# Reordering the first half's triangular substitution in the recurrent block of a two-layer decoder trunk on one core

## The chip, the cores and the metric

The kernel runs on one core of one Trainium2 chip. The metric is the device time of one execution in microseconds (us). Before the change the median of three runs is 2140.88 us (2133.08 to 2142.15).

## What is computed

The program is a trunk of two layers over 512 tokens of width 1024. Each layer is a half SwiGLU block, a mixer and another half SwiGLU block. Layer 0 mixes by attention, layer 1 by RWKV-7. Only the RWKV-7 mixer is touched:

```
xx = shift(h) - h;   xr, xw, xk, xv, xa, xg = [h + xx * mix[i] for i in range(6)]
r, k, v = xr @ w_r, xk @ w_k, xv @ w_v
decay = exp(-exp(-softplus(-(w0 + tanh(xw @ w1) @ w2)) - 0.5));  a = sigmoid(a0 + (xa @ a1) @ a2)
S_t = S_{t-1} (diag(decay_t) - kk_t^T (kk_t * a_t)) + v_t k_t^T;   y_t = S_t r_t      (16 heads of 64)
```

The kernel doesn't step through the tokens. It works in chunks of 64 tokens and, in each chunk and head, needs the inverse of a unit triangular 64 x 64 matrix of "ties" between the chunk's tokens.

## The kernel before

The heads are worked in two halves of eight (`sg` 0 and 1, four head pairs `j` each). Ahead of the recurrence stand three projections, each as two halves of 512 output columns: K, V, R. `project(half, ...)` runs over eight pieces k of the contraction; for k = 0 to 5 it issues 12 matmuls (4 blocks of 128 by 3 split products, L120, tile rm) and yields, then the pieces 6 and 7 block by block with two more yields. These are steps 0 to 7. `weave` resumes side generators after named steps of a projection, so side work sits between the matmuls. Matmuls keep their written order (`pinned`). On the other engines a scheduler orders the instructions by its own timeline, and `after(ins, dep)` adds a constraint of order to it.

The side generators that matter:

- `rw_own_ties` (L1542, L1552): per pair 16 small matmuls (tile rq) make the ties, VectorE masks them into `us`, and the SyncE queue (SP) stores them to DRAM as `lin` in four transfers of 32 KB: 16 for a half.
- `rw_inverse` (L1591 to L1616): SP loads `lin` back as one 512 KB tile with one 32 x 32 triangle per partition, GpSimd presets T, and VectorE substitutes in 31 steps of two operations each (L1601 product, L1607 sum). Then T and its transposed copy U go out to DRAM (ScalarE copy L1616), come back, and two rounds of 32 x 32 matmuls finish the 64 x 64 inverse.
- `rw_decay` (L1492 to L1497): per pair six matmuls into two rq banks (there are three), which ScalarE empties by two tanh (line 102, `us` and `pa`), then a VectorE scan (L1495) and two exponentials on ScalarE (line 102 again).
- `evac_v` (L1356 to L1364): V's eight blocks are copied by ScalarE, centred by GpSimd, and stored by SP as `vd` and `vcd`, 256 KB each.
- `mixed` (L1321 to L1334): makes each token-shifted input piece: ScalarE scale, VectorE add (L1323), ScalarE cast (L1332), and the low part on GpSimd or VectorE (L1334). R mixes its eight pieces anew for each half.

R and K, V weights were split earlier and lie in DRAM; SP loads them back piece by piece (L288, 512 KB each, tile parts) into a ring of four slots. SP issues all of the above in one order, so a transfer that waits holds those behind it. VectorE and ScalarE work in order too.

In the kernel before, the first half's ties come after steps 3 to 6 of V's first half, and the whole of its substitution is resumed after step 7.

Of the kernel before, what the change touches and what calls it, by code (L numbers as in the profile page):

```python
# [14 lines left out]
ALU = mybir.AluOpType  # L15
# [34 lines left out]
class Trunk:  # L50
    def __init__(self, ctx, tc, aps):
        self.tc, self.nc, self.a = tc, tc.nc, aps
        nc = self.nc
        self.cp = ctx.enter_context(tc.tile_pool(name="const", bufs=1))
        self.sb = ctx.enter_context(tc.tile_pool(name="work", bufs=1))
        self.ps = ctx.enter_context(tc.tile_pool(name="banks", bufs=1, space=PSUM))
        self.dram = ctx.enter_context(tc.tile_pool(name="dram", bufs=1, space=DRAM))

        n_x = N_CONST + NCH * S
        self.call, self.cpos = self.cp.tile([P, n_x + 4096], F32, name="const"), 0  # L60
        self.x_all, self.raw_all = self.shaped(self.call[:, N_CONST:n_x], [NCH, S]), self.call[:, n_x:]
        self.parts_all = self.cp.tile([P, 8192], F32R, name="parts")
        self.x = [self.x_all[:, c, :] for c in range(NCH)]
        self.ident = self.c("ident", [P])
        make_identity(nc, self.ident)
        self.ones = self.c("ones", [P], 1.0)

        self.blk = self.c("blk", [P], 0.0)
        for h in range(2):
            nc.gpsimd.memset(self.blk[h * 64 : (h + 1) * 64, h * 64 : (h + 1) * 64], 1.0)  # L70
        self.consts = {}
        self.wlist, self.wring, self.wblocks, self.plan_ring = [], [], [], "f"

        self.wloads, self.slot_last, self.fops, self.n_ffn = [], {}, {}, 0
        self.extra, self.extra_for = None, 0

        self.wkeep = {}

        self.parked_w, self.park_ops, self.park_turn = {}, [], 0
        self.wload = self.wconv = self.wpos = 0  # L80
        self.wcv = {}
        self.n_conv = 0

        self.fcol = self.c("fcol", [4, 4])
        self.conv_ahead, self.limit = 2, 1 << 30
        self.last_mm = self.turned = self.gate = None

        self.pinned, self.last_pe = False, None
        self.parking = False
        self.table, self.table_ins, self.preload = None, [], None  # L90
# [1207 lines left out]
    def rwkv(self, gain):  # L1298
        nc, mm = self.nc, self.nc.tensor.matmul
# [46 lines left out]
        vd = self.dram.tile([4, P, D], F32, name="vd")  # L1346
        vcd = self.dram.tile([4, P, D], F32, name="vcd")

        def evac_v(half, ps):


            e = lambda z: z.rearrange("p (h d) -> p h d", d=C)
            for b in range(4):
                t, tc = self.row("v", 4), self.row("vc", 2)
                mean = self.vmean[:, half, b, :]
                nc.scalar.copy(t, ps[b])  # L1356
                nc.vector.tensor_reduce(out=mean, in_=e(t), axis=AX.X, op=ALU.add)
                nc.scalar.mul(mean, mean, 1.0 / C)
                nc.gpsimd.tensor_tensor(
                    out=e(tc), in0=e(t), in1=mean[:, :, None].to_broadcast([P, 8, C]), op=ALU.subtract  # L1360
                )
                cs = slice(half * S, (half + 1) * S)
                nc.sync.dma_start(vd[b][:, cs], t)
                nc.sync.dma_start(vcd[b][:, cs], tc)  # L1364

        def project(half, xm, evac, natural, i_mix=None):

# [50 lines left out]
        weave(project(0, xm, evac_k, False, 2), ((6, 7), decay))  # L1418
        weave(project(1, xm, evac_k, False), ((0, 1), decay), ((0, 1, 2), norm), ((6, 7), keys))
        xm = {}  # L1420
        ties, norm, inverse = self.rw_own_ties(0), self.rw_norm(1), self.rw_inverse(0, None)
        weave(project(0, xm, evac_v, True, 3), ((0, 1), keys), ((0, 1, 2), norm), ((3, 4, 5, 6), ties), ((7,), inverse))
        weave(project(1, xm, evac_v, True))
        decay, keys, ties = self.rw_decay(1), self.rw_keys(1), self.rw_own_ties(1)
        bonus = []
        evac_r = lambda half, ps: bonus.append(self.rw_prep2(half, ps))

        weave(project(0, None, evac_r, False, 0), ((2, 3, 4, 5), decay), ((6, 7), keys))
        weave(
            project(1, None, evac_r, False, 0),  # L1430
            ((0, 1), keys), ((2, 3, 4, 5), inverse), ((4, 5, 6, 7), ties), ((6, 7), bonus[0]),
        )
        recur = self.rw_recur(0)
        next(recur)
        inverse = self.rw_inverse(1, None)
        weave(recur, ((6, 7), bonus[1]), ((2, 5, 8, 11, 14, 20, 21, 22, 23), inverse))
        self.limit = len(self.wlist)
        self.rw["g2"] = self.next_w()
# [33 lines left out]
    def rw_decay(self, sg):  # L1472
# [5 lines left out]
        for j in range(4):  # L1478
# [13 lines left out]
            nc.scalar.activation(pi, pi, AF.Identity, bias=self.const(1.0))  # L1492
            self.act(self.rw_rate(j), ps[1], AF.Tanh, scale=0.5, bias=col("a0"))
            runs = self.runs.rearrange("p c t -> p (c t)")
            nc.vector.tensor_tensor_scan(out=cum, data0=runs, data1=pi, initial=0.0, op0=ALU.mult, op1=ALU.add)  # L1495
            self.act(pr, cum, AF.Exp, scale=-0.5 * E_HALF)
            self.act(pi, cum, AF.Exp, scale=0.5 * E_HALF)  # L1497
            yield
# [81 lines left out]

    halves = [(slice(h * 64, h * 64 + 64), slice(64 - h * 64, 128 - h * 64)) for h in range(2)]

    def rw_inverse(self, sg, dep):

        nc, mm = self.nc, self.mm
        rw = self.rw
# [2 lines left out]
        inv = self.x_all[:, :4].rearrange("p (n i) s -> p n (i s)", n=2) if sg else self.shaped(self.raw_all[:, :2048], [2, 1024])  # L1589
        L, T, pt = inv[:, 0, :], inv[:, 1, :], self.rows[:, 2:].rearrange("p i s -> p (i s)")  # L1590
        load = nc.sync.dma_start(L, rw["lin", sg])  # L1591
        U, t0, L = L, pt, big(L)
        self.after(nc.gpsimd.memset(T, 0.0), load)
        nc.gpsimd.memset(T[:, 0::33], 1.0)
# [2 lines left out]
        for i in range(31):  # L1597
# [5 lines left out]
                in1=T[:, i : i + 1, :j].to_broadcast([P, n, j]), op=ALU.mult,  # L1603
            )
            if done == 0:
                self.after(ins, self.newed if sg else dep)
            nc.vector.tensor_tensor(out=T[:, j:, :j], in0=T[:, j:, :j], in1=pv, op=ALU.add)  # L1607

            done += 2 * n * j + 250
            if sg and done > 3740:  # L1610
                done = 0
                yield
        dt = self.dram.tile([P, 1024], F32, name=f"tout{sg}")
        du = self.dram.tile([P, 1024], F32, name=f"uout{sg}")
        nc.sync.dma_start(dt.rearrange("p (i t) -> p i t", i=32), T)
# [312 lines left out]
```

## Time and profile before

| | |
|---|---|
| three runs, median (range) | 2140.88 us (2133.08 to 2142.15) |
| profiled execution, its own time | 2135.13 us |
| its span, mean granted TensorE clock | 2133.2 us, 0.987 |
| TensorE busy | 2048.1 us (96%) |
| VectorE busy | 1585.9 us (74%) |
| ScalarE, GpSimd busy | 954.4 us (45%), 123.4 us (6%) |

The profiled execution lies inside the range of the runs, 5.75 us under their median. Times inside it are counted from the span's start. V's projection runs from about 1447 to 1506, R's from about 1504 to 1583; the recurrence follows.

### The profile page before, as it was taken

Reading aid. Unit: us, or ns where it says so; the run is one execution under the profiler, and the core shown is the slowest. Engines: PE = TensorE matmul, PEld = TensorE weight load, DVE = VectorE, ACT = ScalarE, POOL = GpSimd, SP = SyncE. Lnnn points to the kernel's source line nnn. Section 1 sums busy time; section 2 is a strip of 40 time slices with the busy share of each in tenths; the row PEclk is TensorE's granted clock in tenths of the full one; section 3 lists DMA queues with packets and bytes.
Section 4 is the critical chain, followed back from the end, with each engine's and each line's share of the span. In section 5 each row is a group of like instructions: output and inputs, shape, how many; then the busy total and the mean of one; then the engine's idle time right before and its main releaser. Section 6 shows DMA issues by size and latency. Waiting matters only on the chain.

```text
span 2133.2 us, 29169 instructions
## 1 busy us (share of the span) xinstructions
PE 2048.1 (96%) x11527; PEld 1639.8 (77%) x11527; DVE 1585.9 (74%) x1981; ACT 954.4 (45%) x1381; POOL 123.4 (6%) x165
## 2 busy tenths in 40 slices
PE   8999999999989999999999999999898999999998
PEld 6788888776877788877878888777566668888887
DVE  6778786467777888887798888556966557887784
ACT  5433443354335554444544444373634425433342
POOL 0000000211000000000000000112322100000000
PEclk9999999999989999999999999999989999999999
DMA  5333332421113468763255674536654332333321
GB/s 169 89 115 103 99 99 72 125 79 51 52 47 100 147 221 275 237 207 128 62 196 197 211 235 158 207 112 191 213 135 104 91 120 83 109 99 119 109 89 40
DMA packets 219296, 282.41 MB, mean 132 GB/s; under 512 B 45395, under 2 KB 135659, under 8 KB 219160
## 3 DMA queue, kind: packets, MB, share of 16 engines
q1 hardware_dynamic: 216520, 278.20, 41.4%
q10 hardware_dynamic: 2640, 2.36, 0.3%
q8 instruction: 91, 1.49, 0.3%
q14 instruction: 45, 0.37, 0.1%
HBM read 227.76 MB, written 54.59 MB: 132 GB/s over the span
## 4 chain that ended last, share of the span: by engine, by line
PE 77%; DVE 11%; DMA 5%; ACT 3%; issue 2%; SPq 1%; POOL 0%; DVEq 0%; ACTq 0%
PE fp L120 36%; PE fd L120 18%; PE am L120 7%; PE rm L120 4%; PE rq L120 2%; DVE parts L297 2%; PE wo L120 2%; DMA const<-in_ffn_w_up_dram 1%; PE rl L120 1%; PE rr L120 1%; DVE const L1601 1%; DVE wx L293 1%; DVE const L1607 1%; ACT parts L296 1%; PE fd L691 1%
## 5 line engine op out<-in xcount | busy, mean ns | idle before, releaser
L120 PE MATMUL fp<-parts,xs 128*128 128x512 f32 x2016 | 493.1, 393 | 13.2 <-DVE parts L297 9.0
L120 PEld LDWEIGHTS fp<-parts,xs 128*128 128x128 f32 x2016 | 377.6, 189 | 96.6 <-DVE parts L297 12.0
L120 PE MATMUL fd<-act,parts 128*128 128x512 f32 x1728 | 409.4, 390 | 2.5 <-DVE acts L332 1.6
L296 ACT CAST parts<-wx 128x1024 fp32r<-128x1024 f32 x224 | 233.6, 1051 | 349.9 <-PE fp L120 174.6
L120 PEld LDWEIGHTS fd<-act,parts 128*128 128x128 f32 x1728 | 323.7, 188 | 72.6 <-DVE acts L332 3.4
L297 DVE TENSOR_TENSOR parts<-wx,parts 128x1024 fp32r<-128x1024 f32 x224 | 271.8, 1220 | 73.2 <-ACT parts L296 73.1
L296 ACT CAST parts<-const 128x1024 fp32r<-128x1024 f32 (+1 forms) x192 | 198.2, 1033 | 262.0 <-PE fp L120 134.0
L120 PE MATMUL fp<-parts,xb 128*128 128x512 f32 x1152 | 291.3, 400 | 9.6 <-ACT wx L668 6.8
L297 DVE TENSOR_TENSOR parts<-const,parts 128x1024 fp32r<-128x1024 f32 (+1 forms) x192 | 229.5, 1197 | 59.4 <-ACT parts L296 54.3
L120 PEld LDWEIGHTS fp<-parts,xb 128*128 128x128 f32 x1152 | 216.8, 191 | 56.1 <-ACT wx L668 7.4
L654 DVE TENSOR_TENSOR wx<-fp,wx 128x1024 f32<-128x1024 f32 x140 | 168.7, 1218 | 30.0 <-PE fp L120 28.8
L712 DVE SCALAR_TENSOR_TENSOR const<-fd,const 128x512 f32<-128x512 f32 x160 | 108.4, 685 | 77.6 <-PE fd L120 77.4
L120 PE MATMUL fp<-parts,xa 128*128 128x512 f32 x576 | 145.0, 400 | 4.3 <-ACT xa L572 2.6
L120 PEld LDWEIGHTS fp<-parts,xa 128*128 128x128 f32 x576 | 110.2, 193 | 29.2 <-ACT xa L572 3.3
L120 PE MATMUL am<-xg,parts 128*128 128x512 f32 x384 | 99.4, 410 | 0.0
L416 POOL TENSOR_TENSOR ssum<-ssum,sq 128x512 f32<-128x512 f32 x14 | 23.0, 1646 | 1198.3 <-ACT sq L415 1197.9
L120 PEld LDWEIGHTS am<-xg,parts 128*128 128x128 f32 x384 | 72.0, 191 | 25.6 <-issue 9.9
L102 ACT ACTIVATE wx<-wx,const 128x512 f32<-128x512 f32 x80 | 53.5, 716 | 43.7 <-DVE wx L654 43.6
L242 ACT CAST acts<-wx 128x1024 fp32r<-128x1024 f32 (+2 forms) x37 | 37.1, 1004 | 68.4 <-DMA wx<-in_rw_wk_dram 18.3
L243 DVE TENSOR_TENSOR acts<-wx,acts 128x1024 fp32r<-128x1024 f32 (+2 forms) x37 | 42.9, 1162 | 24.5 <-ACT acts L242 24.5
L120 PE MATMUL rm<-xm,parts 128*128 128x512 f32 x252 | 60.8, 394 | 0.0
L331 ACT CAST act<-fd 128x512 fp32r<-128x512 f32 x80 | 43.7, 587 | 37.3 <-PE fd L691 37.1
(316 smaller groups left out, 2632.9 us busy)
## 6 DMA issues: line engine op xcount, KB each, us to landing
wx<-in_ffn_w_down_dram SPq DMA_DIRECT2D x72, 512.0 KB
parts<-acts SPq DMA_DIRECT2D x68, 512.0 KB
parts<-parts SPq DMA_DIRECT2D x68, 512.0 KB
wx<-in_ffn_w_gate_dram SPq DMA_DIRECT2D x44, 512.0 KB
wx<-in_ffn_w_up_dram SPq DMA_DIRECT2D x40, 512.0 KB
const<-in_ffn_w_up_dram SPq DMA_DIRECT2D x40, 512.0 KB
const<-in_ffn_w_gate_dram SPq DMA_DIRECT2D x36, 512.0 KB
const<-in_ffn_w_down_dram SPq DMA_DIRECT2D x16, 512.0 KB
```

The source lines that it names most:

```text
L102: ins = nc.scalar.activation(out, in_, func, **kw)
L120: return self.pe(self.nc.tensor.matmul(*args, **kw))
L242: nc.scalar.copy(hi, src)
L243: nc.vector.tensor_tensor(out=lo, in0=src, in1=hi.bitcast(F32), op=ALU.subtract)
L293: self.nc.vector.tensor_tensor(out=out, in0=in0, in1=in1, op=ALU.add)
L296: self.last_cast = self.nc.scalar.copy(hi[:r, :n], raw[:, :n])
L297: self.nc.vector.tensor_tensor(out=lo[:r, :n], in0=raw[:, :n], in1=hi[:r, :n].bitcast(F32), op=ALU.subtract)
L331: self.nc.scalar.copy(hi, t)
L416: nc.gpsimd.tensor_tensor(out=ssum, in0=ssum, in1=sq, op=ALU.add)
L654: add = lambda out, other, ps=ps: nc.vector.tensor_tensor(out=out, in0=ps, in1=other, op=ALU.add)
L691: nc.tensor.transpose(ps[:, b * P : (b + 1) * P], us[n][b][:, f * P : (f + 1) * P], self.ident)
L712: nc.vector.scalar_tensor_tensor(out=self.x[c], in0=ps, scalar=0.5, in1=self.x[c], op0=ALU.mult, op1=ALU.add)
```

## The change

Four edits. (1) The ties of the first half come after steps 2 to 5 of V's first half, one step sooner, and the substitution is resumed after step 6. (2) V's stores are put behind the load of the substitution's input by constraints of order (`behind`). (3) The substitution of the first half yields after step i = 24, and its last six steps (25 to 30) are resumed in R's first half after step 2, right behind the first decay pair, and tied behind that pair's scan (`scanned`). (4) The argument `dep`, always None, goes.

```
-                nc.sync.dma_start(vd[b][:, cs], t)
-                nc.sync.dma_start(vcd[b][:, cs], tc)
+                self.after(nc.sync.dma_start(vd[b][:, cs], t), self.behind)
+                self.after(nc.sync.dma_start(vcd[b][:, cs], tc), self.behind)
...
-        weave(project(0, xm, evac_v, True, 3), ((0, 1), keys), ((0, 1, 2), norm), ((3, 4, 5, 6), ties), ((7,), inverse))
+        weave(project(0, xm, evac_v, True, 3), ((0, 1), keys), ((0, 1, 2), norm), ((2, 3, 4, 5), ties), ((6,), inverse))
...
-        weave(project(0, None, evac_r, False, 0), ((2, 3, 4, 5), decay), ((6, 7), keys))
+        weave(project(0, None, evac_r, False, 0), ((2, 3, 4, 5), decay), ((2,), inverse), ((6, 7), keys))
...
-            nc.vector.tensor_tensor_scan(out=cum, ...)
+            self.scanned = nc.vector.tensor_tensor_scan(out=cum, ...)
...
         load = nc.sync.dma_start(L, rw["lin", sg])
+        if not sg:
+            self.behind = load
...
             if done == 0:
-                self.after(ins, self.newed if sg else dep)
+                self.after(ins, self.newed if sg else self.scanned if i else None)
...
-            if sg and done > 3740:
+            if done > 3740:
                 done = 0
-                yield
+                if sg or i == 24:
+                    yield
```

The lines below L1589 move down by three to four in the changed file: L1601, L1607 and L1616 become L1604, L1610 and L1620.

The SP queue at the end of V's first half, before (`lin` stores L1552, weights L288, V's stores L1363 and L1364, the substitution's load L1591):

```order
L1363 DMA vd<-v 128x512
L1552 DMA lin_9854<-us 32x8x32
L1363 DMA vd<-v 128x512
L1364 DMA vcd<-vc 128x512
L1552 DMA lin_9854<-us 32x8x32 x2
L1364 DMA vcd<-vc 128x512
L288 DMA parts<-parts_6282 128x1024
L1552 DMA lin_9854<-us 32x8x32 x2
L288 DMA parts<-parts_6282 128x1024
L1363 DMA vd<-v 128x512 x2
L288 DMA parts<-parts_6372 128x1024
L1591 DMA const<-lin_9854 128x1024
```

The same place in the change:

```order
L1552 DMA lin_9837<-us 32x8x32 x8
L288 DMA parts<-parts_6188 128x1024
L1552 DMA lin_9837<-us 32x8x32 x4
L288 DMA parts<-parts_6188 128x1024
L1552 DMA lin_9837<-us 32x8x32 x4
L1591 DMA const<-lin_9837 128x1024
L1363 DMA vd<-v 128x512 x2
L288 DMA parts<-parts_6282 128x1024 x2
L1364 DMA vcd<-vc 128x512
L1363 DMA vd<-v 128x512
```

The load stood behind six of V's stores and three weight pieces, of which three V stores and one weight piece lay between the `lin` stores themselves; now it stands right behind the last `lin` store, and the two pieces `parts_6282` stand behind the load.

VectorE around the first decay scan (L1495) of R's first half, before:

```order
L1607 TENSOR_TENSOR const<-const 128x13x19
L1601 TENSOR_TENSOR const<-const 128x240
L1495 SCALAR_TENSOR_TENSOR heads<-const,us 128x512
L1607 TENSOR_TENSOR const<-const 128x12x20
L1323 SCALAR_TENSOR_TENSOR const<-const 128x511
L1601 TENSOR_TENSOR const<-const 128x231
```

And in the change:

```order
L1610 TENSOR_TENSOR const<-const 128x8x24
L1604 TENSOR_TENSOR const<-const 128x175
L1610 TENSOR_TENSOR const<-const 128x7x25
L1495 SCALAR_TENSOR_TENSOR heads<-const,us 128x512
L1604 TENSOR_TENSOR const<-const 128x156
L1323 SCALAR_TENSOR_TENSOR const<-const 128x511
```

Before, the scan was queued in the middle of step 19; now it is queued after the whole of step 24. Between the first product and this scan lie the same other VectorE operations in both: seven L1323, one L1334 and four L1357.

ScalarE in R's first half, after the tanh of the second decay pair, as a piece of the difference (L1620 is the copy U, the two lines 102 behind it the tanh of the third pair):

```order
 L1492 ACTIVATE us<-us,const 128x512
 L1321 ACTIVATE const<-const 128x512 x2
+L1620 COPY const<-const 128x1024
 L102 ACTIVATE us<-rq,const 128x512
 L102 ACTIVATE pa<-rq,const 128x512
```

The copy U, which stood behind all four pairs' tanh and the first copy of R's banks, now stands ahead of the third pair's.

## Rows read from the trace of the kernel before

**Rows 1.** TensorE's waits, 1440 to 1590: total us, times, longest.
```profile
PE rq L120 <- ACT us L102: 4.3, 2, 3.5
PE rm L120 <- POOL parts L1334: 2.6, 2, 1.5
PE rm L120 <- DMA parts<-parts: 2.2, 2, 1.6
PE rm L120 <- ACT r L1560: 1.4, 3, 0.6
PE rm L120 <- ACT parts L1332: 1.3, 1, 1.3
```

**Rows 2.** A stretch: us, busy PE, PEld, DVE, ACT, POOL; granted clock, DMA share, GB/s.
```profile
1560.00:1570.00 10.00, 10.00 (x182) 7.84 (x180) 5.50 (x10) 2.84 (x5) 3.53 (x3) 0.79 0.35 86
```

**Rows 3.** Chain of waits, 1456 to 1560: start, us, what.
```profile
1474.70 4.72 DMA parts<-parts
...
1482.67 4.19 DMA lin<-us
...
1486.93 6.01 DMA const<-lin
...
1542.29 2.58 POOL xm L1334
1544.86 1.68 POOL parts L1334
```

**Rows 4.** Chain of waits, 1400 to 1800: the second half's store and load.
```profile
1586.69 5.29 DMA lin<-us
1592.04 3.63 DMA const<-lin
```

**Rows 5.** SP in order of time: start, us, engine, line, transfer, count.
```profile
1469.42 1.81 SPq L1552 DMA_DIRECT2D lin<-us  x4
...
1481.73 0.37 SPq L288 DMA_DIRECT2D parts<-parts  x1
```

**Rows 6.** VectorE in order of time; in brackets the idle time before, and its releaser.
```profile
1476.67 0.68 DVE L1542 TENSOR_TENSOR us<-rq,const 128x512 f32<-128x512 f32 x1
...
1493.06 0.19 DVE L1601 TENSOR_TENSOR const<-const 128x31 f32<-128x31 f32 x1 [10.23 <-DMA const<-lin]
...
1496.17 1.26 DVE L1601 TENSOR_TENSOR const<-const 128x112 f32<-128x112 f32 x1
1497.46 0.28 DVE L1607 TENSOR_TENSOR const<-const 128x112 f32<-128x112 f32 x1
...
1521.89 1.23 DVE L1495 TENSOR_TENSOR_SCAN heads<-const,us 128x512 f32<-128x512 f32 x1
...
1524.42 0.40 DVE L1607 TENSOR_TENSOR const<-const 128x231 f32<-128x231 f32 x1
...
1536.82 0.19 DVE L1607 TENSOR_TENSOR const<-const 128x31 f32<-128x31 f32 x1
```

**Rows 7.** ScalarE in order of time.
```profile
1525.23 0.68 ACT L102 ACTIVATE us<-rq,const 128x512 f32<-128x512 f32 x1
...
1537.94 2.09 ACT L1616 COPY const<-const 128x1024 f32<-128x1024 f32 x1
```

**Rows 8.** TensorE in order of time.
```profile
1519.01 3.02 PE L120 MATMUL rm<-xm,parts 128*128 128x512 f32 x12
...
1525.96 1.12 PE L120 MATMUL rq<-hids,parts 64*128 64x512 f32 x5 [3.50 <-ACT us L102]
1527.01 4.42 PE L120 MATMUL rm<-parts 128*128 128x512 f32 x12
1531.36 0.96 PE L120 MATMUL rq<-hids,parts 64*128 64x512 f32 x6
...
1546.59 4.38 PE L120 MATMUL rm<-parts 128*128 128x512 f32 x11 [1.50 <-POOL parts L1334]
...
1558.42 5.06 PE L120 MATMUL rm<-parts 128*128 128x512 f32 x11 [1.12 <-POOL parts L1334]
```

More of the change, by code (lines that the diff above doesn't have):

```diff
@@ L85, in __init__ @@
         self.conv_ahead, self.limit = 2, 1 << 30
-        self.last_mm = self.turned = self.gate = None
+        self.last_mm = self.turned = self.gate = self.behind = None
         self.pinned, self.last_pe = False, None
@@ L1420, in rwkv @@
         xm = {}
-        ties, norm, inverse = self.rw_own_ties(0), self.rw_norm(1), self.rw_inverse(0, None)
-        weave(project(0, xm, evac_v, True, 3), ((0, 1), keys), ((0, 1, 2), norm), ((3, 4, 5, 6), ties), ((7,), inverse))
+        ties, norm, inverse = self.rw_own_ties(0), self.rw_norm(1), self.rw_inverse(0)
+        weave(project(0, xm, evac_v, True, 3), ((0, 1), keys), ((0, 1, 2), norm), ((2, 3, 4, 5), ties), ((6,), inverse))
         weave(project(1, xm, evac_v, True))
@@ L1434, in rwkv @@
         next(recur)
-        inverse = self.rw_inverse(1, None)
+        inverse = self.rw_inverse(1)
         weave(recur, ((6, 7), bonus[1]), ((2, 5, 8, 11, 14, 20, 21, 22, 23), inverse))
@@ L1494, in rw_decay @@
             runs = self.runs.rearrange("p c t -> p (c t)")
-            nc.vector.tensor_tensor_scan(out=cum, data0=runs, data1=pi, initial=0.0, op0=ALU.mult, op1=ALU.add)
+            self.scanned = nc.vector.tensor_tensor_scan(out=cum, data0=runs, data1=pi, initial=0.0, op0=ALU.mult, op1=ALU.add)
             self.act(pr, cum, AF.Exp, scale=-0.5 * E_HALF)
@@ L1581, with rw_inverse @@
     halves = [(slice(h * 64, h * 64 + 64), slice(64 - h * 64, 128 - h * 64)) for h in range(2)]
-    def rw_inverse(self, sg, dep):
+    def rw_inverse(self, sg):
         nc, mm = self.nc, self.mm
```

## Prediction

> **What bounds the kernel now.** TensorE is busy for 96% of the span, so time can only be won where it waits or runs at a lower clock. I read first its waits around the change [rows 1]: between 1440 and 1590 it waits 4.3 us for ScalarE's tanh of the decay pairs, 2.6 and 1.3 us for R's mixed pieces, 2.2 us for weights and 1.4 us for R's banks, 11.8 us in all. Then the stretches [rows 2]: from 1560 to 1570 TensorE's granted clock is 0.79 of full speed after the waits before it, that is, it ran part of the time at the lower of its two levels. Then the chain of waits [rows 3]: it leaves TensorE for a weight piece (4.72 us), the last `lin` store (4.19 us) and the substitution's load (6.01 us), and from there runs through VectorE. VectorE stood idle 10.23 us for that load [rows 6], and ended the last step at 1537.0. The 43.9 us from 1493.06 to there hold the decay scans, the mixing and the substitution in one queue, and most of TensorE's waits hang on something in that queue.
>
> So the place is a stall of VectorE, paid for by TensorE 30 to 65 us later. What an earlier start is worth is not the shift itself, but what it takes out of those waits.
>
> **The load.** Ties one step sooner: a step of V is 12 matmuls, 3.02 us in a later row of the same shape [rows 8]. The fourth pair's mask, at 1476.67 [rows 6], can thus run about 3 us sooner and end near 1474.3. TensorE's work is only permuted. On SP four `lin` stores take 1.81 us [rows 5]. The third pair's are out by about 1475, the weight piece that follows by 1476, then the last four. Before, the third of these waited for a weight piece to land: in the chain the piece's 4.72 us end at 1479.42, just ahead of the store [rows 3]. The same kind of wait (SP keeps only so many transfers open) ties it now to the other piece of that pair, issued near 1472.5, so about 1477.2. The last store is issued by 1478.1, where before it was 1482.7.
>
> How long the store then takes to land isn't shown for this mix. Before it took 4.19 us with V's stores and a weight piece ahead [rows 3], in the second half 5.29 us [rows 4]. Only one weight piece is ahead of it now, so it can be well under 4.19; 2.5 and 5.3 are my ends, and I take 4.0. The load took 6.01 us with the same crowd ahead of it [rows 3], and 3.63 us in the second half, without V's stores [rows 4]. The change puts it in the second situation: 3.7 us, with 6.0 as the upper end. It lands near 1486 (between 1484.3 and 1489.4), against 1492.94: 7 us sooner.
>
> The Trainium skill (DMA: Bandwidth & Descriptors, "Queues, rings and completion order") says that each DMA engine takes up descriptors in ring order. By that rule V's stores and the weights, issued behind the load, can't lengthen it, and the lower price stands; were they shared evenly, it would be the 6.01 us, the load would land at 1488.3, and the gain below would lose its first term.
>
> What pays: the two pieces `parts_6282`, issued at 1481.73 before [rows 5], stand behind the load's wait and two V stores, near 1483.5, and TensorE waits for the first. Of its 2.2 us for weights [rows 1] I make 3 to 3.5. This costs nothing as long as the decay wait behind it is longer than the difference, since that wait is set by VectorE and not by TensorE's arrival.
>
> **From the load to the first scan.** Before, 28.8 us of queue lie between the first product and the first decay scan (1493.06 to 1521.89 [rows 6]). The same other operations lie there now, plus the rest of step 19 and steps 20 to 24, eleven operations of about 0.40 us [rows 6]: 4.3 us. Two of GpSimd's subtractions for V, which ran before while VectorE stood idle, now fall beside the substitution. What one costs is shown by the product of 112 elements, 1.26 us beside a GpSimd operation, where the sum of the same size took 0.28 [rows 6]: 1.0 each, 2 us. So 28.8 + 4.3 + 2 = 35.1 us, and the scan runs at 1521.1, not 7 but 0.8 us sooner. The part of the substitution put ahead of the scan eats the shift. With a load at 1484.3 it is 2.5 us sooner, with 1489.4 it is 2.6 us later.
>
> TensorE's wait of 3.50 us for the second pair's tanh [rows 8] ends when ScalarE, after the scan, has done two exponentials, two casts and that tanh: from 1521.89 to the tanh at 1525.23 [rows 7]. It stays, ending 0.8 to 1.5 us sooner. The slow stretch behind it (12 matmuls in 4.42 us instead of 3.02 [rows 8]) stays as well.
>
> The last six steps come out of the queue 4 us after the scan, near 1526, where they ended at 1537 before [rows 6]. The copy U (2.09 us [rows 7]) then stands ahead of the third pair's tanh on ScalarE; it can't start before 1526 and holds that tanh until 1529 or 1530, which costs the fourth pair's matmuls up to 1 us. So the end of the decay matmuls (1531.36 + 0.96 before [rows 8]) moves by only **-1.0 us**. Ends: -5 if the decay waits go (4.3 [rows 1] and a part of the slow stretch), +3 with the late load and the copy in full.
>
> **R's second half.** Here I expect most of the gain. Before, the copy U stood in front of the copies of R's banks (1537.94 [rows 7]), and VectorE was behind with everything. Now the substitution is out of the way some 10 us earlier.
> - R's bank copies: 1.4 us of waits [rows 1], of which the copy U makes a part: **-0.5** (0 to -1.4).
> - The wait of 1.50 us at 1546.59 [rows 8]: GpSimd made the third piece first (2.58 us) and then the second (1.68 us), on which TensorE waited [rows 3]. In the changed order the second piece's cast stands ahead of the third's on ScalarE: **-1.5** (0 to -1.5).
> - The waits for the fourth piece, 1.3 for its cast and 1.12 for GpSimd's part [rows 1, 8]: VectorE reaches that piece some 6 us sooner, TensorE by 3 to 4: **-2.4** (-0.5 to -2.4).
> - The clock: 11 matmuls took 4.38 and again 5.06 us behind these waits [rows 8], where 11/12 of 3.02 is 2.77: 3.9 us lost. If the waits go the clock has no reason to fall; I leave a quarter: **-3.0** (-1 to -3.9).
>
> Behind it, ties, inverse and recurrence of the first half hang on TensorE, and the second half's substitution on the ties; I let the shift pass through whole. The results of the first inverse come back some 10 us sooner than they are asked for, which nobody waits for. Sum: -1.0 - 0.5 - 1.5 - 2.4 - 3.0 = **-8.4 us**. Ends: -14 with all best, about +2 with all worst. From the profiled 2135.13 us this gives 2126.7. That execution was 5.75 us under the median of the runs, so against the median it is **2132.5 us**, 0.4% less. About 0.5% (10.7 us) is what a measurement can tell from no change.
>
> **Rivals.**
> - *All of it goes.* The load lands at 1484.3 or before and the decay wait nearly disappears, with its slow stretch: -14 us, 2127 against the median. For it speaks that the wait is set by one queue; against it that the added steps stand ahead of the scan. 0.22.
> - *Only the front moves.* R's second half is bound by VectorE's keys and mixing and ScalarE's order anyway, and as the waits are taken out of one place they return at the next piece: -3 us, 2138. For it speaks that ScalarE, with casts, exponentials, bank copies and a table load, is in one queue. 0.22.
> - *The copy and the load in the way (slower).* The `lin` store takes 5.3 us and the load 6.0, so it lands at 1489.4. The scan is then 2.6 us late, the last steps end at 1528, the copy U holds ScalarE until 1531, and the fourth pair's matmuls and then every cast of the second half stand behind it. That is +3 at the end of the decays; the waits of the second half stay, as ScalarE now is the late one, and V's weights behind the load add 2 to 3 us of wait, of which the late scan hides most: +4, 2145. It decides at a load near 1487: from there the scan is later than before. 0.12.
> - That the load doesn't move can be excluded: the queue shows it right behind the last store.
>
> **How the numbers follow.** The forecast (-6 to -11) has 0.44. Faster by over 0.5% are the first rival and the upper edge of the forecast, 0.22 + 0.09 = 0.31. Slower by over 0.5% needs more than twice the slow rival's sum; I give it half that rival's chance, 0.06, for costs that no row shows. Within 0.5%: 0.63. For the range, the lower end is the first rival's gain of 14 taken from the profiled execution, 2121; the upper end is no gain against the median, and 1 us for the small side of the slow rival: 2142. Outside lie most of the slow rival and a little of the first, 0.15 together.
>
> **What would show it.** Right: the substitution's first product near 1486; 128x7x25 just ahead of the first scan at about 1521; a TensorE wait of 2 to 3.5 us left at the second decay pair; no wait over 0.5 us for R's pieces in the second half, and a granted clock near 1.0 there; the recurrence starting 8 us sooner. Wrong: a first product after 1488, a wait for weights in V of over 4 us, the copy L1620 named as the one that TensorE's decay matmuls wait for, or waits for pieces moved to the fifth or sixth.

## The result and the profile after

The changed kernel is slower: 2151.81 us median of 9 runs (2144.67 to 2155.26) beside 2141.82 us (2133.08 to 2145.51) for the kernel before in the same comparison, a ratio of 1.0048 [1.0036, 1.0059]. Forecast was a gain of 8.4 us; measured is a loss of 10.

The profiled execution of the change took 2154.63 us with a span of 2152.7. I cut both spans at the first matmul of V (tile rm from weights as the stationary side), the first of the recurrence (ra) and the first of the projection behind it (wo). Before, then after (duration in ns min/median/max, first and last start in us):

```profile
L120 PE MATMUL rm<-parts,xm x192: 388/389/501, 1447.2 to 1503.6; 128*128 128x512 f32 x192
...
L120 PE MATMUL ra<-heads x512: 269/269/472, 1586.7 to 1704.7; 64*64 64x128 f32 x171
...
L120 PE MATMUL wo<-z,parts x192: 388/389/504, 1712.9 to 1774.3; 128*128 128x512 f32 x192
```

```profile
L120 PE MATMUL rm<-parts,xm x192: 387/389/796, 1451.5 to 1511.8; 128*128 128x512 f32 x192
...
L120 PE MATMUL ra<-heads x512: 269/269/472, 1590.8 to 1722.8; 64*64 64x128 f32 x171
...
L120 PE MATMUL wo<-z,parts x192: 388/389/793, 1731.5 to 1794.0; 128*128 128x512 f32 x192
```

V and R together took 139.5 us before and 139.3 after; the recurrence took 126.2 and now 140.7; the rest 420.3 and 421.2. The 4.3 us by which V starts later lie in code that the change doesn't touch. So nothing was won where the change works, and 14.5 us were lost behind it, in a place where no line of the diff stands. (The two profiled executions differ by 19.5 us and the medians by 10: the profile of before lies 6.7 us under its median, that of the change 2.8 over.)

**The recurrence.** TensorE's waits there, with the longest now:

```profile
PE rr L120 <- DMA const<-vcd: 7.3, 2, 7.2
```

It waits for `vcd`, the centred V of the first half's last chunk (L1671; L1667 before), and TensorE's own row shows the same:

```profile
1493.14 19.03 PE L120 MATMUL rm<-parts,xm 128*128 128x512 f32 x72 [4.18 <-DMA parts<-parts]
...
1534.63 0.96 PE L120 MATMUL rq<-hids,parts 64*128 64x512 f32 x5 [1.38 <-ACT us L102]
...
1563.68 4.12 PE L120 MATMUL rm<-parts 128*128 128x512 f32 x11 [5.04 <-POOL parts L1334]
...
1649.09 0.44 PE L120 MATMUL rr<-const 64*64 64x64 f32 x2 [7.17 <-DMA const<-vcd]
```

Why the load is late stands in SP's order. Before, it went out right behind the store of T (the second half's substitution); then T was loaded back, U stored and loaded back:

```profile
1630.54 0.34 SPq L1615 DMA_DIRECT2D tout<-const  x1
1630.99 1.25 SPq L1667 DMA_DIRECT2D const<-vcd  x2
1633.38 0.93 SPq L1622 DMA_DIRECT2D const<-tout  x2
1634.36 0.70 SPq L1617 DMA_DIRECT2D uout<-const  x1
1638.05 2.17 SPq L1632 DMA_DIRECT2D us<-uout  x4
```

After, the same pair of loads (each 64 KB) is queued behind the whole round trip:

```profile
1635.12 0.34 SPq L1619 DMA_DIRECT2D tout<-const  x1
1638.30 0.94 SPq L1626 DMA_DIRECT2D const<-tout  x2
1639.33 0.51 SPq L1621 DMA_DIRECT2D uout<-const  x1
1644.36 2.12 SPq L1636 DMA_DIRECT2D us<-uout  x4
1646.52 1.26 SPq L1671 DMA_DIRECT2D const<-vcd  x2
```

The reload of U at 1644.36 can't be issued before U's store at 1639.33 has landed, which by the chain of waits took 5.01 us; the pair, which needs neither, stands behind it. It was issued 0.45 us after T's store before, and is issued 11.4 us after it now. The stretches of the same profile (us, busy PE, PEld, DVE, ACT, POOL; granted clock, DMA share, GB/s) show what the wait drags behind it:

```profile
1490.00:1500.00 10.00, 6.86 (x20) 5.49 (x21) 8.69 (x23) 0.00 (x0) 2.38 (x2) 0.66 1.07 386
...
1560.00:1570.00 10.00, 6.32 (x80) 5.03 (x81) 9.91 (x15) 2.67 (x6) 5.31 (x2) 0.67 0.12 33
...
1650.00:1660.00 10.00, 10.00 (x266) 9.34 (x264) 2.04 (x3) 2.84 (x6) 0.00 (x0) 0.50 0.30 87
1660.00:1670.00 10.00, 9.87 (x211) 8.04 (x207) 3.76 (x7) 5.94 (x13) 1.05 (x1) 0.72 0.53 160
```

From 1650 to 1660 the granted clock is 0.50, the lower level (1.2 GHz) throughout, and 0.72 in the next stretch. What both come to is read from the recurrence as a whole, before and after:

```profile
1586.70:1712.90 126.20, 107.67 (x2349) 81.74 (x2348) 75.89 (x144) 56.95 (x139) 26.36 (x30) 0.99 0.36 99
```

```profile
1590.80:1731.50 140.70, 116.84 (x2350) 89.92 (x2349) 75.35 (x144) 57.24 (x139) 26.02 (x29) 0.89 0.32 89
```

TensorE stands idle 23.9 us where it was 18.5, 5.3 us more (the 7.3 us wait came, smaller waits went), and is busy 9.2 us longer with the same matmuls at a mean clock of 0.89 instead of 0.99. That makes the 14.5 us. So the larger part of the loss is not the wait itself but the matmuls at the lower level. Not all of them stand right behind the wait for the pair: from 1680 to 1690 the clock is at 0.66 too, behind a wait of 2.67 us that the kernel before has as well (2.66), there at 1.00.

**V and R.** TensorE's waits from 1440 to 1590, which answer to [rows 1]:

```profile
PE rm L120 <- POOL parts L1334: 5.0, 1, 5.0
PE rm L120 <- DMA parts<-parts: 4.2, 1, 4.2
PE rq L120 <- ACT us L102: 1.9, 2, 1.4
PE rm L120 <- POOL xm L1334: 1.3, 1, 1.3
PE rm L120 <- ACT xm L1332: 0.2, 1, 0.2
```

The sum is 12.6 us; before it was 12.4, since the 11.8 us of the prediction leave out a wait of 0.6 us for V's banks. The decay wait and the waits for R's banks went (4.3 to 1.9, 1.4 to nothing), and as much came back as a wait for V's weights and one for R's fourth piece. The last four stores and the load, VectorE, ScalarE and GpSimd, for the steps below:

```profile
1480.59 1.84 SPq L1552 DMA_DIRECT2D lin<-us  x4
...
1486.02 4.42 DMA const<-lin
```

```profile
1490.56 0.19 DVE L1604 TENSOR_TENSOR const<-const 128x31 f32<-128x31 f32 x1 [5.69 <-DMA const<-lin]
...
1524.35 0.34 DVE L1610 TENSOR_TENSOR const<-const 128x175 f32<-128x175 f32 x1
1524.84 1.23 DVE L1495 TENSOR_TENSOR_SCAN heads<-const,us 128x512 f32<-128x512 f32 x1
...
1531.72 0.19 DVE L1610 TENSOR_TENSOR const<-const 128x31 f32<-128x31 f32 x1
...
1556.24 0.74 DVE L1323 SCALAR_TENSOR_TENSOR const<-const 128x511 f32<-128x511 f32 x1
...
1557.56 0.73 DVE L1323 SCALAR_TENSOR_TENSOR const<-const 128x511 f32<-128x511 f32 x1
...
1562.53 0.68 DVE L1647 COPY const<-rq 32x512 f32<-32x512 f32 x1
```

```profile
1531.95 2.05 ACT L1620 COPY const<-const 128x1024 f32<-128x1024 f32 x1
```

GpSimd's subtraction for R's fourth piece, which ends TensorE's wait of 5.0 us, and the one that ended its wait of 1.12 us in the kernel before:

```profile
1557.76 5.86 POOL L1334 TENSOR_TENSOR parts<-const,parts 128x512 fp32r<-128x512 f32 x1 [5.12 <-ACT parts L1332]
```

```profile
1556.82 1.54 POOL L1334 TENSOR_TENSOR parts<-const,parts 128x512 fp32r<-128x512 f32 x1 [2.53 <-ACT parts L1332]
```

ScalarE's cast for the same piece in the kernel before, and what stood ahead of it:

```profile
1555.52 0.58 ACT L1643 COPY const<-rq 32x512 f32<-32x512 f32 x1 [2.67 <-PE rq L120]
1556.12 0.62 ACT L1332 CAST parts<-const 128x512 fp32r<-128x512 f32 x1
```

### The profile page after: what moved, and what is told of

Read it like the earlier page. It is cut to its first block, busy times and chain, and to the rows that moved or that the text cites. A ratio compares the mean times of both kernels' runs of the same rounds, so it can differ in the third digit from the quotient of the medians.

```text
span 2152.7 us, 29166 instructions
## 1 busy us (share of the span) xinstructions
PE 2059.7 (96%) x11527; PEld 1652.0 (77%) x11527; DVE 1588.9 (74%) x1981; ACT 954.8 (44%) x1381; POOL 128.1 (6%) x165
## 4 chain that ended last, share of the span: by engine, by line
PE 76%; DVE 11%; DMA 6%; ACT 4%; issue 2%; SPq 1%; POOL 0%; DVEq 0%; ACTq 0%; POOLq 0%
PE fp L120 36%; PE fd L120 17%; PE am L120 7%; PE rm L120 4%; PE rq L120 3%; DVE parts L297 2%; PE wo L120 2%; PE rr L120 1%; DMA const<-in_ffn_w_up_dram 1%; PE rl L120 1%; DVE wx L293 1%; ACT parts L296 1%; DVE const L293 1%; DVE const L1610 1%; DVE const L1604 1%
## 5 line engine op out<-in xcount | busy, mean ns | idle before, releaser
L296 ACT CAST parts<-const 128x1024 fp32r<-128x1024 f32 (+1 forms) x192 | 198.2, 1033 | 259.7 <-PE fp L120 138.3
```

The costliest lines, as they stand in the source:

```text
L296: self.last_cast = self.nc.scalar.copy(hi[:r, :n], raw[:, :n])
```

## The experiments

Theory: the ties, one step sooner, shift the scheduler's timeline so that it queues the pair behind the round trip, and that is the loss; V and R stay as they were because VectorE's order puts R's pieces where they stood. Rivals: the loss is in V and R after all (the weights behind the load, the copy U, GpSimd late), or the recurrence suffers from the split. Every kernel was timed in five rounds; ratios are to the kernel before on the same chip. V+R and recurrence are of the one profiled execution, and a difference of two us in them tells nothing: the kernel before, e3 and e4 queue the same operations in the same order up to the recurrence and took 139.5, 137.6 and 138.4 us for V and R. Nor do sixteen intervals of which some end at 1.0000 or just beside it prove a difference.

| run | median us | ratio [95%] | V+R | recurrence |
|---|---|---|---|---|
| the change | 2151.81 | 1.0048 [1.0036, 1.0059] | 139.3 | 140.7 |
| e1_pair_first | 2144.32 | 1.0011 [0.9999, 1.0024] | 139.2 | 125.4 |
| e3_before_pair_last | 2147.88 | 1.0029 [1.0012, 1.0045] | 137.6 | 136.2 |
| e4_split_only | 2144.27 | 1.0006 [0.9993, 1.0020] | 138.4 | 125.4 |
| e5_no_split_pair_first | 2142.21 | 0.9998 [0.9984, 1.0011] | 137.7 | 134.1 |
| e6_piece_on_vector | 2144.10 | 1.0008 [0.9995, 1.0021] | 139.0 | 135.0 |
| e7_weights_first | 2144.09 | 1.0010 [0.9994, 1.0026] | 140.4 | 131.2 |
| e8_both | 2144.81 | 1.0001 [0.9987, 1.0015] | 140.1 | 128.4 |
| e10_ties_only | 2151.83 | 1.0040 [1.0026, 1.0054] | 138.5 | 141.4 |
| e11_mix_early | 2142.57 | 0.9996 [0.9978, 1.0014] | 135.8 | 131.7 |
| e12_before_mix_early | 2140.97 | 0.9984 [0.9971, 0.9998] | 138.3 | 128.7 |
| e13_weights_mix | 2141.41 | 0.9986 [0.9972, 1.0000] | 136.9 | 128.7 |
| e14_no_split_mix | 2141.41 | 0.9983 [0.9968, 0.9998] | 135.3 | 131.5 |
| e15_u_first | 2139.39 | 0.9988 [0.9970, 1.0006] | 135.5 | 128.5 |
| e16_after_u_first | 2150.23 | 1.0034 [1.0015, 1.0053] | 139.5 | 137.5 |
| e17_before_mix_u_first | 2143.08 | 1.0001 [0.9986, 1.0016] | 137.9 | 128.3 |

### The pair

**e1_pair_first**: the change, with the round trip's other transfers ordered behind the pair.

```diff
-        nc.sync.dma_start(du, U)
+        self.back = [nc.sync.dma_start(du, U)]
...
-            nc.sync.dma_start(t0[lo], src)
+            self.back.append(nc.sync.dma_start(t0[lo], src))
...
+            if not sg and c == NC - 1:
+                for ins in self.back:
+                    self.after(ins, vin)
```

> The changed kernel with one thing put back: the last two vcd loads of the first half's recurrence stand on SP ahead of the reloads of T and the store and reloads of U of the second half's inverse, as they did before the change; nothing else in any engine's order differs from the changed kernel. Theory 'pair' (TensorE's 7.2 us wait for these loads, and the half clock behind it, are the loss): the wait for const<-vcd is gone, the recurrence from the first ra matmul to the first wo matmul takes 126 to 129 us instead of 140.7, and the time is within 4 us of the kernel before. Rival 'front' (the loss is V's weights held behind the substitution's load, 4.2 us of wait with a slow stretch, and the 5.0 us wait for GpSimd's piece): the time stays 7 to 11 us above the kernel before.

The wait for the pair is gone, the recurrence took 125.4 us, and the ratio fell from 1.0048 to 1.0011: 0.0037, or 7.9 of the 10 us. In the two traces every engine works in the same order but for this pair on SP, so the rest of the change is the same in both.

**e3_before_pair_last**: the kernel before, with nothing but the pair moved behind the reload of U.

```diff
-                nc.sync.dma_start(dst, src)
+                self.us_back = nc.sync.dma_start(dst, src)
...
+            if not sg and c == NC - 1:
+                self.after(vin, self.us_back)
```

> The kernel before with the last two vcd loads of the first half's recurrence put behind the first reload of U of the second half's inverse. Theory 'pair': TensorE waits 5 to 8 us for const<-vcd, runs the next 10 us at about half clock, and the time is 8 to 13 us above the kernel before, though V and R are untouched. Rival 'front': no more than 2 us above.

The order became one `us` reload, the pair, three reloads, and TensorE waits:

```profile
PE rr L120 <- DMA const<-vcd: 3.4, 2, 3.0
```

Recurrence 136.2 us, ratio 1.0029: without any other part of the change, one displaced pair costs 6.2 us. Wait and time are both below what was expected (5 to 8 and 8 to 13 us); the pair stands behind one reload of U here and behind all four in the change.

**e10_ties_only**: of the change only `((2, 3, 4, 5), ties), ((6,), inverse)`; no order for V's stores, no split.

> Of the change only the ties one step sooner with the resumption after step 6; no order behind the load, the substitution in one piece. If the earlier ties by themselves make the scheduler queue the last pair of centred-V loads behind the second round trip, and that is the loss: the wait for that pair is 3 to 7 us in two pieces, the recurrence takes 134 us or more instead of 126, and the time is 2147 to 2152. If the loss needs the split or the order behind the load: no wait for the pair over 1 us, recurrence 125 to 127, 2139 to 2144.

The wait is 7.5 us in one piece, the recurrence 141.4 us, the ratio 1.0040. The ties with the earlier resumption displace the pair without the other two edits; its place in the source didn't change, only what the scheduler made of it.

**e4_split_only**: of the change only the last six steps behind the first scan.

> The kernel before with only the last six steps of the first half's substitution put behind the first decay scan; the ties stay a step later and V's stores are not tied. The vcd pair stands where it stood before. Theory 'pair': no wait for const<-vcd, and the time is within 6 us of the kernel before, either way. Rival 'front' expects the weights of V as before (2.2 us of wait) and nothing over 3 us lost; a rival 'split' (the copy U ahead of the third pair's tanh is the loss) expects 5 us or more lost.

No wait for the pair, recurrence 125.4 us, no difference from before. But this kernel doesn't test the split. With the ties in their old place the last six steps stood behind the first scan anyway, and the copy U stayed behind the decays (at 1544.21); the trace has every engine in the order of the kernel before:

```profile
1527.70 0.41 DVE L1604 TENSOR_TENSOR const<-const 128x240 f32<-128x240 f32 x1
1528.17 1.23 DVE L1495 TENSOR_TENSOR_SCAN heads<-const,us 128x512 f32<-128x512 f32 x1
1529.31 0.38 DVE L1610 TENSOR_TENSOR const<-const 128x240 f32<-128x240 f32 x1
```

So its 1.0006 is the kernel before, measured once more. That the loss doesn't need the split is shown by e10; what the split is worth in the change is seen only between e1 and e5 (1.0011 and 0.9998, with intervals that overlap), and isn't settled.

**e16_after_u_first**: the change, with the store of U ahead of the reload of T in the second half, one swap on SP.

```diff
-        nc.sync.dma_start(du, U)
+        uo = nc.sync.dma_start(du, U)
...
-            nc.sync.dma_start(t0[lo], src)
+            self.after(nc.sync.dma_start(t0[lo], src), uo if sg else None)
```

> The changed kernel with the same swap and nothing else; the pair stays behind the round trip. Theory A (the pair waits for the round trip ahead of it): the wait for the pair falls from 7.2 by 1 to 2 us and the time from 2152 to 2148 to 2150, still above the kernel before. If the pair's own transfers are slow whatever stands ahead: the wait stays at 7 us and the time at 2152.

Its SP rows, and TensorE's wait:

```profile
1640.20 3.35 SPq L1636 DMA_DIRECT2D us<-uout  x4
1643.60 1.24 SPq L1671 DMA_DIRECT2D const<-vcd  x2
```

```profile
PE rr L120 <- DMA const<-vcd: 4.2, 2, 3.8
```

Counted from T's store, U's store is issued 2.2 us sooner (2.0 us behind it instead of 4.2) and the pair 3.2 us (8.2 instead of 11.4), and the wait shrinks by 3.1, more than the 1 to 2 expected. The time (1.0034) can't be told from that of the change. So the pair waits for what stands ahead of it in the queue; its own transfer isn't slow.

### V and R

**e5_no_split_pair_first**: the change without the split, pair first (the loss then being at most that of the ties and of V's stores).

> Ties a step sooner and the load ahead of V's stores, the substitution not split, and the vcd pair put back as in the first run. Theory 'pair': no wait for const<-vcd; the time is within 6 us of the kernel before, and tells from the first run what the split is worth. From the original reasoning (scan late behind the substitution): the load lands 3 to 5 us sooner than in the kernel before, the scan 3 to 5 us sooner, and the time is 3 to 8 us below the kernel before. Rival 'front': V's weights wait 3 us or more, and the time is above the kernel before.

Same as before in time (0.9998), V+R 137.7. The gain of 3 to 8 us that the prediction's reasoning expected of it didn't come.

**e6_piece_on_vector**: e1, and the low part of the piece that TensorE waits 5 us for made by VectorE.

```diff
-            eng = nc.vector if i == 2 or i == 0 and c == 0 else nc.gpsimd
+            eng = nc.vector if i == 2 or i == 0 and (c == 0 or n == 28) else nc.gpsimd
```

> This is the changed kernel with the displaced pair ahead of the round trip (as in the run of that name), plus one edit: the low part of the piece of R's second half that TensorE waited 5 us for (the 28th mixed piece) is made by VectorE instead of GpSimd. Theory A (GpSimd, sharing a port with VectorE, was kept out of it by VectorE's back-to-back operations on two inputs): the 5.1 us wait for GpSimd's part goes, the next piece's on GpSimd takes its place with at most 2 us, the clock in that stretch is near 1.0; V and R together take 134 to 137 us instead of 139.2, and the time falls by 3 to 5 us against the pair-first kernel (2139 to 2141). Theory B (VectorE itself is the late one, and GpSimd only the last in its chain): the wait stays at 4 us or more, now named for VectorE or a cast of ScalarE, and the time stays within 1.5 us of 2144.

The wait stayed and changed its name; GpSimd, with the next piece only, is slow all the same:

```profile
PE rm L120 <- DVE parts L1334: 4.6, 1, 4.6
```

```profile
1555.56 5.15 POOL L1334 TENSOR_TENSOR parts<-const,parts 128x512 fp32r<-128x512 f32 x1 [7.71 <-ACT parts L1332]
```

Theory B came: VectorE's own product was queued behind seven others and was as late as GpSimd's. But GpSimd's lateness in the change is more than VectorE's order (see the fourth piece, below): its subtraction took 5.86 us where it took 1.54 before. So handing the piece to VectorE trades one for the other.

**e7_weights_first**: e1, and the two pieces `parts_6282` ahead of the substitution's load.

```diff
-            self.nc.sync.dma_start(parts[:r, :, :n].bitcast(F32), self.parked_w.pop(i))
+            self.lead(self.nc.sync.dma_start(parts[:r, :, :n].bitcast(F32), self.parked_w.pop(i)))
...
+    def lead(self, piece):
+        if self.behind is not None and self.ahead:
+            self.ahead -= 1
+            self.after(self.behind, piece)
```

> The pair-first kernel plus one edit: the first two weight pieces of V's second half are queued ahead of the substitution's load instead of behind it. Theory A (the 4 to 5 us wait for weights in V, with the lower clock behind it, is the price of putting the load ahead, and no cover hides it): the wait falls to 0 to 2 us, the load lands no more than 1.5 us later, V and R together take 3 to 5 us less than 139.2, time 2139 to 2141. Theory B (as forecast: the wait costs nothing since the decay wait behind it is set by VectorE): the wait falls but the decay waits grow by as much (from 2.4 to 5 or more), V and R take within 1.5 us of 139.2, time within 1.5 us of 2144.

The weights' wait fell from 5.0 to 1.1, the decay wait rose from 2.4 to 4.4, a wait of 1.5 for V's banks came up, and V+R took 140.4. The weights behind the load have no cost that can be told (1.0010 beside 1.0011 in e1), as forecast.

**e8_both**: e6 and e7 together.

> The two edits before together on the pair-first kernel. If each wait is a cost of its own: V and R together 131 to 134 us, 5 to 9 us under the pair-first kernel, 2135 to 2139, below the kernel before by 3 to 7. If a wait taken out of one place returns at the next: 136 to 139 us, and a time within 3 us of 2142.

V+R 140.1, time as in e1 within the intervals: the waits taken out came back.

**e11_mix_early**: e1, and by constraints of order VectorE mixes the third and fourth piece of R's second half ahead of some of the products of R's banks and of the keys.

```diff
-            nc.vector.scalar_tensor_tensor(
+            add = nc.vector.scalar_tensor_tensor(
...
-            )
+            ); [self.after(self.rw[late], add) for late in EARLY.get(n, ())]
...
+EARLY = {
+    27: (("rp", 0, 1), ("rk", 0, 1), ("kx", 1, 1)),
+    28: (("rp", 0, 3), ("rk", 0, 3), ("kk", 1, 2), ("kx", 1, 1)),
+}
```

(`rp` and `rk` are the two operations of L1565 and L1566, `kk` and `kx` those of L1513 and L1516, kept under those names.)

> The pair-first kernel plus one edit: by constraints of order VectorE mixes the third and fourth piece of R's second half (the 27th and 28th mixed piece) ahead of the products of R's banks and of the third and fourth pair's keys, so the fourth piece is mixed some 4 us sooner; nothing is added or taken away. Theory A (the stall in R's second half is the place of the fourth piece in VectorE's queue, and the 6 us that the load gained are lost because that place did not change): TensorE's waits of 2.4 and 5.1 us there fall to 3 us or less together, the stretch from V's start to the recurrence shrinks from 139.2 to 133 to 136 us, time 2138 to 2141. Theory B (the wait returns at the next piece, or as a wait of the ties for the delayed keys): the stretch stays at 138 or more and the time within 1.5 us of 2144.

```profile
PE rm L120 <- POOL parts L1334: 2.4, 2, 1.7
```

The waits for these pieces fell from 7.5 us (5.1 and 2.4) to 2.4, and V+R from 139.2 to 135.8, while the waits for weights (4.8) and for the decays (2.7) stayed and one of 2.1 us for VectorE (tile us) came up. So these pieces set more of the time there than the weights do. Two things changed at once: the fourth piece was mixed 101.7 us after V's start in place of 104.3, and GpSimd's subtraction for it took 2.2 us in place of 5.86; the run doesn't tell them apart. The ratio went from 1.0011 to 0.9996, within the intervals, and the time is above the 2138 to 2141 us expected.

**e12_before_mix_early**, **e13_weights_mix**, **e14_no_split_mix**: the same constraints in the kernel before, in e7, and in e5.

> The same constraint in the kernel before, without any part of the change. Theory A: its waits for the fourth piece (1.3 and 1.1 us) go, and some of the slow stretch behind them: V and R together 136 to 138 us instead of 139.5, time 2 to 4 us less than before. Theory B (return elsewhere): no difference over 1 us.

> The weights-first kernel plus the same constraint. There the wait for weights was taken away and came back as 4.4 us at the decay pairs, with the fourth piece's 5.4 and 2.4 still behind. Theory A: the fourth piece's waits go, V and R together take 133 to 137 us, time 2138 to 2141. Theory B: 138 us or more, no difference over 1.5 us against 2144.

> The kernel with the ties sooner, V's stores behind the load, no split and the pair first (2142.2 so far), plus the same constraint. If the waits for the second half's pieces are VectorE's order, V and R together fall from 137.7 to 133 to 136 us and the time to 2136 to 2140, under the kernel before; if they return, the time stays at 2141 to 2144.

V+R 138.3, 136.9 and 135.3, times 0.9984, 0.9986 and 0.9983 of the kernel before, 3.0 to 3.6 us less, with intervals that end at 1.0000 or just under it. These are the best versions found; what they gain is less than the 0.5% named in the prediction, and e17 and e15, built on e12 and e14, came out at 1.0001 and 0.9988, so that the gain isn't sure. The 138.3 of e12 can't be told from the kernel before.

**e15_u_first**, **e17_before_mix_u_first**: the swap of e16 in e14 and in e12.

> The no-split kernel with early mixing plus one swap on SP: in the second half the store of U goes ahead of the reload of T, so it is issued as soon as GpSimd's copy is done, some 1.8 us sooner, and U comes back as much sooner. Theory A (the rest of the loss is the late landing of the round trip, behind which TensorE runs at its lower clock): no wait over 0.9 us before the second round of the second inverse, granted clock 1.0 from 1645 to 1665, recurrence 124 to 127 us instead of 131.5, time 2136 to 2139. Theory B (something else): recurrence 130 or more, time within 1 us of 2141.4.

> The kernel before with the early mixing and the same swap. Theory A: recurrence 124 to 127 us in the profile instead of 128.7, and 2 to 4 us less time than the early mixing alone: 2137 to 2139 beside 2142 to 2144 for the kernel before. Theory B: no difference over 1 us from the early mixing alone.

Recurrences of 128.5 and 128.3 us and no gain in time that can be told from none: both expectations of 124 to 127 failed. So the swap isn't worth having where the pair stands in its place. That the recurrence took between 125.4 and 135.0 us in kernels with the pair in its place isn't explained by the round trip alone, and stays open; so do the 2.4 us (1.0011, an interval that includes none) that the change would still lose with the pair in its place.

## Why the prediction was wrong

**The step that failed** is the sentence "Behind it, ties, inverse and recurrence of the first half hang on TensorE, and the second half's substitution on the ties; I let the shift pass through whole." It took the recurrence's order for fixed and so put nothing into the sum for it. The schedule there is made anew from a timeline that the ties had shifted (that the timeline is the reason is argued; that the ties with the earlier resumption suffice, e10 shows), and two loads of 64 KB moved behind a round trip that they don't need: +14.5 us in the profile, 7.9 of the 10 us by e1, 6.2 with the pair alone (e3), 8.6 with the ties and the earlier resumption alone (e10). The order of SP shows this move before any run, as the pair's row behind the reload of U; the prediction read the queues in V and R alone, and all its rivals lay there too.

**Point by point**, times from V's start (1447.2 before, 1451.5 after). The sum had a second step that failed, the one on the fourth piece.

- *The load.* Forecast 7 us sooner; the first product ran 45.9 us after V's start before [rows 6] and 39.1 after: 6.8 sooner. The last store was issued 30.5 us after V's start (forecast 30.9) and the load 4.0 us behind it, as taken; the load took 4.42 (taken: 3.7, with 6.01 as the other end), with two of V's stores and two weight pieces issued right behind it. Over all kernels its time goes by what stands ahead: 4.0 to 4.5 us in the nine with no weight piece queued between the last store and the load, 5.0 to 6.0 in the eight with two there, e7 among them (6.02). The Trainium skill (DMA: Bandwidth & Descriptors, "Queues, rings and completion order") says that each DMA engine takes up descriptors in ring order, and this agrees; that what stands behind adds nothing isn't shown, since all nine lie above the 3.48 to 3.88 of the second half.
- *The first scan.* Forecast 0.8 us sooner, with the added steps eating the shift: 74.7 before [rows 6], 73.3 after, 1.4 sooner; the row of 128x175 (step 24's sum has 128x7x25 elements) stands just ahead of it, as forecast.
- *The end of the decay matmuls.* Forecast -1.0: 85.1 us after V's start before [rows 8], 84.1 after (1534.63 + 0.96). That this is right to the tenth is luck. The decay waits were to stay and went from 4.3 to 1.9, and the slow stretch behind them (4.42 us for 12 matmuls) went too; but TensorE came to these matmuls 3.0 us later after V's start, through the weights' wait. The copy U at 1531.95 stood in the way less than allowed for.
- *V's weights.* Forecast a wait of 3 to 3.5 us that costs nothing; it was 4.2, with a granted clock of 0.66 in that stretch; e7, without most of it, is no faster.
- *R's bank copies and the second piece.* -0.5 and -1.5: both waits are gone, but the third piece has one of 1.3.
- *The fourth piece and the clock.* -2.4 and -3.0: here the step "VectorE reaches that piece some 6 us sooner" failed. The substitution did end 9.4 us sooner after V's start (1531.72 beside 1536.82), but the mixing operations of the fourth and fifth piece stand at 1556.24 and 1557.56, 104.7 and 106.1 us after V's start; before, the pair of them began at 104.2. What was won had gone into VectorE's idle time and into products of R's banks and keys, which the scheduler ranked ahead. So nothing was gained at this piece; the wait became 5.0 us, and the clock 0.67 in place of 0.79 [rows 2], by something that the prediction had no term for: GpSimd's subtraction took 5.86 us in place of 1.54, so 4.3 of the 5.0 us are that (the last section). Nor had VectorE set the waits at this piece before: it was done with both pieces by 1552.8, and the cast that TensorE waited for stood on ScalarE behind a copy which waited for TensorE itself (the rows of ScalarE above). e11, which mixes the third and fourth piece sooner, gives 3.4 us of V+R.
- So the rival "only the front moves" was the one that V and R went by (waits taken out of one place returned at the next piece), with nothing left of its 3 us; the loss came from a place that no rival named.

## What to carry to other kernels

Where a scheduler sets the order from its own timeline, an edit can reorder queues far from the diff: compare every engine's whole order, DMA queues first, and look at each transfer that has slipped behind one that waits for a landing. A load that depends on nothing near it should be tied to its place by a constraint. The same comparison tells whether an experiment changes anything at all: e4 didn't. And a stall that is removed upstream only pays if the order of the late engine hands the time to what the bounding engine waits for next; if that operation keeps its place in the queue, the time ends as idle time in between.

## What was not expected of the hardware

**GpSimd beside VectorE.** In the change the subtraction at 1557.76 took 5.86 us, in e6 one took 5.15 us at 1555.56, where the same form otherwise takes 1.3 to 1.9 us. In both VectorE ran operations with two inputs back to back, some 0.68 us each, until a copy with one input came up. The Trainium skill (SBUF — State Buffer, "SBUF: two separate sides") says that the two share a port as an exclusive lock: whichever starts first holds it for its whole instruction and the other blocks. By that rule a wait of one operation, 0.7 us, would be expected; the rows show 3 to 4.5 us more than usual, the time of five to seven, as if the waiting side didn't get the next turn. When it gets one, the rows do show: in the change VectorE's copy starts at 1562.53 and GpSimd ends at 1563.62, 1.1 us later; in e6, e1, e7, e8 and e16 it also ends 1.1 us after the start of that copy, and in the kernel before too, where the copy (1557.27) came right behind and the subtraction took 1.54. This fits a GpSimd that is kept out until VectorE's run of two-input operations is broken, however long that run is. No run here isolates it.

**The same wait, two clocks.** e1 and e13 wait 0.88 us at the same point of the second inverse. First e1, then e13, TensorE's row and a stretch behind it:

```profile
1648.07 0.50 PE L120 MATMUL rq<-us,const 32*32 32x32 f32 x20 [0.88 <-issue]
```

```profile
1650.00:1660.00 10.00, 8.28 (x205) 6.39 (x199) 4.09 (x7) 6.19 (x15) 1.42 (x2) 1.00 0.70 208
```

```profile
1645.57 0.51 PE L120 MATMUL rq<-us,const 32*32 32x32 f32 x21 [0.88 <-issue]
```

```profile
1648.00:1650.00 2.00, 2.00 (x72) 1.94 (x72) 0.00 (x0) 1.97 (x5) 0.00 (x0) 0.50 0.58 181
```

Behind the same wait TensorE stayed at the higher level in e1 and fell to the lower one (0.50) in e13; the recurrences took 125.4 and 128.7 us. e11, with a wait of 1.52 us there, had 0.60 in the next 10 us and 131.7 us. So the length of the wait at that point doesn't decide by itself whether the clock falls, and a recurrence of one profiled execution can differ by some us for that alone. What decides it stays open.
